# An mLSTM layer on one Trainium2 core: column blocks of the projections taken in pairs, five of eight k chunks by Strassen's seven products

## The chip, the cores and the metric

The kernel runs on one core of one Trainium2 chip. The metric is the device time of one execution in microseconds, as the median of several runs. Lower is better. The kernel before takes 1814.12 us (three runs, 1814.03 to 1814.68).

## The reference

One residual layer for 256 rows (tokens) of 4096 float32 numbers. The rows are normalised by their root mean square, multiplied by w_in (4096 x 16400), and the columns of the product are q and k (8 heads of 256 each), v, og and z (8 heads of 512 each) and 16 gate columns. After a small causal convolution on q and k comes an mLSTM step per head; its result is normalised, gated by sigmoid(og) and silu(z), multiplied by w_out (4096 x 4096) and added to x.

```
u = rms_norm(x) @ w_in
qk, v, og, z, ig, fg = split(u)                 # 2*2048, 4096, 4096, 4096, 8, 8 columns
q, k = silu(causal_conv(qk))                    # 8 heads of 256
a = exp(decay) * (q @ k.T) / 16                 # per head, causal
h = (a @ v) / max(|sum(a)|, exp(-m))            # 8 heads of 512
y = rms_norm_per_head(h) * w * sigmoid(og) * silu(z)
out = x + y @ w_out
```

Nearly all of the arithmetic is the two projections: 256 x 4096 x 20496 multiplications.

## The kernel before

Rows are two tiles of 128 (t = 0, 1), the 4096 of the contraction are 32 k tiles of 128, in 8 chunks of 4 (CK). Float32 accuracy is kept by splitting each operand into a high and a low part of 12 bits (`split`, lines 127 to 130: the high part is a copy on ACT, the low part a subtraction on DVE) and by three matmuls for each product (`matmul3`, lines 132 to 136: high x high, high x low, low x high).

`project` (line 165) computes one block of 512 columns (NB): for each chunk it loads 4 k tiles of weights by SP's DMA (1 MB, three buffers), splits two k tiles at a time (128 x 1024, lines 129 and 130, three buffers each of high and low parts), and issues 24 matmuls for them on TensorE. A block of 512 columns is 192 matmuls with 512 columns each, into two PSUM banks. The split x (the stationary side) stays in SBUF for the whole of w_in. The blocks come in the order of `column_blocks` (line 42): og and z of two heads, then q, k and v of the pair of heads. The first two blocks are computed side by side while x comes in; two blocks (gq, 272 columns, and q1, 256) and the last two of w_out (256) are narrow. In all there are 38 blocks of 512 columns, 31 of w_in (the first two among them) and 7 of w_out, and 4 narrow ones.

Work on finished blocks (convolution, `head` with its stages weights, values and turn, the gates) is put into a queue `stages`, and one stage is issued after each chunk of the blocks that follow. y goes through TensorE transposes into `yT` and is split by `split_y` to be the stationary side of w_out. The tile framework fixes the order of each engine's instructions before the run: where an instruction isn't ready by the framework's own reckoning it puts a later one ahead. Each engine then works in that fixed order.

Of the kernel before, what the change touches and what calls it, by code (L numbers as in the profile page):

```python
# [28 lines left out]
COLS = 2 * QK + 3 * INNER + 2 * HEADS  # L29
# [4 lines left out]
VW = DV + 2  # L34
CK = 4
SK = 2
WARM = 8
NPAIR = HEADS // 2
OUT_BLOCKS = [NB] * 7 + [NB // 2] * 2


def column_blocks():
    """Blocks of w_in's columns in the order in which they are used: (what, head or pair, spans)."""
    o_v, o_og, o_z, o_g = 2 * QK, 2 * QK + INNER, 2 * QK + 2 * INNER, 2 * QK + 3 * INNER
    blocks = []
# [12 lines left out]
    return blocks
# [3 lines left out]
def mlstm_layer(ctx: ExitStack, tc: tile.TileContext, x, xT, norm_w, w_in, conv_w, conv_b, gate_b,  # L62
# [3 lines left out]
    act_in = ctx.enter_context(tc.tile_pool(name="act_in", bufs=1))  # L66
    wpool = ctx.enter_context(tc.tile_pool(name="wpool", bufs=3))
    work = ctx.enter_context(tc.tile_pool(name="work", bufs=2))
    small = ctx.enter_context(tc.tile_pool(name="small", bufs=1))
    ps_pj = ctx.enter_context(tc.tile_pool(name="ps_pj", bufs=4, space=PSUM))  # L70
    ps_a = ctx.enter_context(tc.tile_pool(name="ps_a", bufs=2, space=PSUM))
    ps_n = ctx.enter_context(tc.tile_pool(name="ps_n", bufs=2, space=PSUM))

# [5 lines left out]
    # The array's clock rises while it is busy: products that nothing reads, until the first operands are there.  # L79
    idle = ps_n.tile([P, P], F32, name="idle", tag="n")  # L80
# [4 lines left out]
    # tri[s, t] = 1 where s <= t  # L85
# [4 lines left out]
    # maskT[s, t] = 0 where key s of a tile may be seen by query t of that tile and of the next  # L90
# [5 lines left out]
    nc.vector.tensor_scalar(nid, ident[:HEADS, :HEADS], -1.0, None, op0=OP.mult)  # L96

# [17 lines left out]
    def rsqrt(dst, src, n, tag):  # L115
        """dst = src ** -0.5 for [P, n] of positive float32."""
# [10 lines left out]
    def split(hi, lo, src):  # L127
        """src as hi + lo, each of 12 bits."""
        nc.scalar.activation(hi, src, AF.Copy)  # L129
        nc.vector.tensor_sub(lo, src, hi.bitcast(F32))  # L130

    def matmul3(ps, a, b, first=True, last=True):
        """ps (+)= a.T @ b of float32 operands given as (hi, lo)."""
        nc.tensor.matmul(ps, a[0], b[0], start=first, stop=False)  # L134
        nc.tensor.matmul(ps, a[0], b[1], start=False, stop=False)  # L135
        nc.tensor.matmul(ps, a[1], b[0], start=False, stop=last)  # L136

    # Work on finished blocks, in stages that are issued between the chunks of the blocks that follow.
    stages = deque()

    yT = act_in.tile([P, KT, T], F32, name="yT")

# [1 line left out]
    rstd = const.tile([P, NT], F32, name="rstd")  # L144
    ss_part = const.tile([P, NT, 4], F32, name="ss_part")

    def row_squares(t, c):
        xr = work.tile([P, D // 4], F32, name=f"xr_{t}_{c}", tag="G")
        nc.sync.dma_start(xr, x[t * P:(t + 1) * P, c * (D // 4):(c + 1) * (D // 4)])
        nc.scalar.activation(xr, xr, AF.Square, accum_out=ss_part[:, t, c:c + 1])  # L150

    def row_stats():
# [3 lines left out]
        rsqrt(rstd, ss, NT, "row")  # L156

# [1 line left out]
    def split_x(raw, hi, lo, c, j):  # L159
        s = nw[:, c * CK + j:c * CK + j + 1]  # L160
        nc.scalar.activation(hi[:, j, :], raw[:, j, :], AF.Copy, scale=s)
        nc.vector.scalar_tensor_tensor(lo[:, j, :], raw[:, j, :], s, hi[:, j, :].bitcast(F32),
                                       op0=OP.mult, op1=OP.subtract)

    def project(name, w, off, widths, lhs, start=False, between=None, end=False):
        """Column blocks of w side by side, from off on; returns the psum tiles of each."""
        ps = [[pool.tile([P, NB], F32, name=f"pj_{name}_{b}_{t}", tag=tag)[:, :width] for t in range(NT)]
              for b, (width, (pool, tag)) in enumerate(zip(widths, ((ps_pj, "pj"), (ps_n, "n"))))]
        for c in range(KT // CK):
            # k tiles that are loaded and split together; the first ones are small, to begin early  # L170
            loads = [(0, CK)]
            if start and c < 2:
                loads = [(0, 1), (1, SK), (SK, CK)] if c == 0 else [(0, SK), (SK, CK)]
            raws = []
            for b, width in enumerate(widths):
                raw = wpool.tile([P, CK, NB], F32, name=f"w_{name}_{b}_{c}", tag="wraw")
                raws.append(raw.rearrange("p a b -> p (a b)")[:, :CK * width])
            if start:
                xraw = work.tile([P, CK, T], F32, name=f"xT_{c}", tag="G")
                xsplit = [act_in.tile([P, CK, T], F32R, name=f"x{part}_{c}", tag=f"{part}{c}")  # L180
                          for part in ("hi", "lo")]
                lhs.append(xsplit)
            for a, z in loads:
                if start:
                    nc.sync.dma_start(xraw[:, a:z, :], xT[:, c * CK + a:c * CK + z, :])
                for b, width in enumerate(widths):
                    o = off + D * sum(widths[:b]) + c * CK * P * width + a * width
                    nc.sync.dma_start(raws[b][:, a * width:z * width],
                                      bass.AP(tensor=w.tensor, offset=w.offset + o,
                                              ap=[[CK * width, P], [1, (z - a) * width]]))  # L190
            n = 1 if start and c == 0 else SK * NB // max(widths) // 2 * 2
            for k0 in range(0, CK, n):
                if start:
                    for j in range(k0, k0 + n):
                        split_x(xraw, *xsplit, c, j)
                for b, width in enumerate(widths):
                    hi = wpool.tile([P, SK, NB], F32R, name=f"wh_{name}_{b}_{c}_{k0}", tag="whi")
                    lo = wpool.tile([P, SK, NB], F32R, name=f"wl_{name}_{b}_{c}_{k0}", tag="wlo")
                    hi, lo = (u.rearrange("p a b -> p (a b)")[:, :n * width].rearrange("p (a b) -> p a b", a=n)
                              for u in (hi, lo))  # L200
                    split(hi, lo, raws[b].rearrange("p (a b) -> p a b", a=CK)[:, k0:k0 + n, :])
                    order = [(j, t) for j in range(n) for t in range(NT)]
                    for j, t in sorted(order, key=lambda jt: jt[1]) if end else order:
                        k = k0 + j
                        a = [lhs[c][part][:, k, t * P:(t + 1) * P] for part in range(2)]
                        matmul3(ps[b][t], a, (hi[:, j, :], lo[:, j, :]), c == 0 and k == 0,
                                c == KT // CK - 1 and k == CK - 1)
            if between is not None:
                between(c)
            if stages:  # L210
                stages.popleft()()
        return ps

# [1 line left out]
    gate = {}  # L215

    def gates(ps):
# [23 lines left out]
        def sums():  # L241
            pB = ps_a.tile([P, NT, HEADS], F32, name="pB", tag="a")
# [6 lines left out]
        def maxima():  # L249
            pc = ps_a.tile([HEADS, T], F32, name="pc", tag="a")  # L250
# [6 lines left out]
        def floor():  # L257
            pm = ps_a.tile([P, NT, HEADS], F32, name="pm", tag="a")
# [5 lines left out]
        return [take, forget, sums, maxima, floor]  # L264

# [1 line left out]
    def conv_qk(ps, dst, i0, ct0, n):  # L267
        """ps[t]: [P, n * 128], the columns from ct0 * 128; dst: (hi, lo), [P, .., T], filled from i0."""
# [124 lines left out]
    for n, (what, who, spans) in enumerate(blocks):  # L393
        width = sum(w for _, w in spans)

        def between(c, n=n):
            if n == 0 and c >= 4:
                for t in range(NT):
                    row_squares(t, c - 4)
# [99 lines left out]
```

## Time and profile before

| | |
|---|---|
| median of 3 runs | 1814.12 us |
| span of the profiled execution, first to last instruction | 1812.6 us (1.5 us less than the median) |
| TensorE (PE) busy | 1805.7 us, 8474 matmuls |
| VectorE (DVE) busy | 965.0 us |
| ScalarE (ACT) busy | 848.8 us |
| GpSimd (POOL) busy | 9.4 us |
| moved by DMA | 354 MB, mean 195 GB/s |
| granted TensorE clock, mean | 0.999 |

How to read it: a busy time is the sum of the durations that the profiler gives, without overlaps, so an engine whose busy time is near the span leaves no room. Durations of matmuls overlap (a matmul of 512 columns is shown with 389 ns, but the next one starts after 227 ns), and so, less, do those of DVE and ACT. What an instruction costs its engine is therefore read from the distance of starts where several stand back to back.

### The profile page before, as it was taken

The numbers are of one execution on the slowest core, as the hardware profiler recorded it, in microseconds if no ns is written. First come the engines' busy times: TensorE is split into PE (matmuls) and PEld (weight loads), VectorE is DVE, ScalarE is ACT, GpSimd is POOL, SyncE is SP. The second block draws the span as 40 slices with busy tenths as digits, with TensorE's granted clock in tenths as the row PEclk, the third lists the DMA queues.
The fourth block names the chain that finished last, engine by engine and source line by source line (L and its number), as shares of the span: only waits on it lengthen the run. The fifth ranks groups of instructions, "written<-read, shape, count | busy, mean of one in ns | idle before, by whom it ended". The sixth has DMA issues, their size and how long they took to land.

```text
span 1812.6 us, 20931 instructions
## 1 busy us (share of the span) xinstructions
PE 1805.7 (100%) x8474; PEld 1510.6 (83%) x8474; DVE 965.0 (53%) x1133; ACT 848.8 (47%) x994; POOL 9.4 (1%) x24
## 2 busy tenths in 40 slices
PE   9999999999999999999999999999999999999999
PEld 7888988888888888888888888888888888888889
DVE  5644656554544665545456655454466754444443
ACT  6643545454444454444445544444445653333332
POOL 0000000000000000000000000000000000000000
PEclk9999999999999999999999999999999999999999
DMA  8854655545555555455555544555555466665654
GB/s 311 277 204 176 200 187 186 181 168 188 199 193 188 190 181 185 164 197 196 187 196 194 175 176 172 200 185 195 200 186 185 171 225 209 219 222 203 213 187 141
DMA packets 57089, 354.07 MB, mean 195 GB/s; under 512 B 6944, under 2 KB 8352, under 8 KB 18592
## 3 DMA queue, kind: packets, MB, share of 16 engines
q1 hardware_dynamic: 55584, 348.80, 54.8%
q0 software_dynamic: 1120, 3.67, 0.5%
q8 instruction: 66, 1.08, 0.2%
q10 hardware_dynamic: 288, 0.26, 0.0%
q14 instruction: 31, 0.25, 0.0%
HBM read 348.51 MB, written 4.19 MB: 195 GB/s over the span
## 4 chain that ended last, share of the span: by engine, by line
PE 99%; DMA 0%; SPq 0%; ACT 0%; DVE 0%; issue 0%
PE pj_v L135 7%; PE pj_o L136 6%; PE pj_o L134 6%; PE pj_o L135 6%; PE pj_v L136 6%; PE pj_v L134 6%; PE pj_og L135 6%; PE pj_og L134 6%; PE pj_og L136 6%; PE pj_z L135 6%; PE pj_z L136 6%; PE pj_z L134 6%; PE pj_k L135 3%; PE pj_k L134 3%; PE pj_k L136 3%; PE pj_q L135 3%
## 5 line engine op out<-in xcount | busy, mean ns | idle before, releaser
L130 DVE TENSOR_TENSOR wl_o<-w_o,wh_o 128x1024 fp32r<-128x1024 f32 x128 | 156.8, 1225 | 174.6 <-ACT wh_o L129 174.6
L129 ACT ACTIVATE wh_o<-w_o 128x1024 fp32r<-128x1024 f32 x128 | 135.8, 1061 | 206.8 <-PE pj_o L136 206.0
L130 DVE TENSOR_TENSOR wl_z<-w_z,wh_z 128x1024 fp32r<-128x1024 f32 x112 | 137.2, 1225 | 167.4 <-ACT wh_z L129 167.4
L130 DVE TENSOR_TENSOR wl_v<-w_v,wh_v 128x1024 fp32r<-128x1024 f32 x128 | 156.7, 1224 | 116.3 <-ACT wh_v L129 115.4
L135 PE MATMUL pj_o<-wl_o,yh 128*128 128x512 f32 (+1 forms) x576 | 210.5, 366 | 0.0
L136 PE MATMUL pj_o<-wh_o,yl 128*128 128x512 f32 (+1 forms) x576 | 210.5, 366 | 0.0
L130 DVE TENSOR_TENSOR wl_og<-w_og,wh_og 128x1024 fp32r<-128x1024 f32 x112 | 137.1, 1225 | 135.9 <-ACT wh_og L129 135.4
L129 ACT ACTIVATE wh_v<-w_v 128x1024 fp32r<-128x1024 f32 x128 | 135.6, 1060 | 154.6 <-PE pj_v L136 136.1
L135 PE MATMUL pj_v<-wl_v,xhi 128*128 128x512 f32 x512 | 202.4, 395 | 0.0
L136 PE MATMUL pj_v<-wh_v,xlo 128*128 128x512 f32 x512 | 199.9, 391 | 0.0
L129 ACT ACTIVATE wh_z<-w_z 128x1024 fp32r<-128x1024 f32 x112 | 118.8, 1061 | 169.5 <-PE pj_z L136 146.2
L129 ACT ACTIVATE wh_og<-w_og 128x1024 fp32r<-128x1024 f32 x112 | 118.8, 1060 | 160.7 <-PE pj_og L136 141.7
L134 PE MATMUL pj_o<-wh_o,yh 128*128 128x512 f32 (+1 forms) x576 | 193.3, 366 | 0.0
L134 PE MATMUL pj_v<-wh_v,xhi 128*128 128x512 f32 x512 | 183.7, 391 | 0.0
L135 PE MATMUL pj_og<-wl_og,xhi 128*128 128x512 f32 x448 | 175.0, 391 | 0.0
L136 PE MATMUL pj_og<-wh_og,xlo 128*128 128x512 f32 x448 | 174.4, 389 | 0.0
L135 PE MATMUL pj_z<-wl_z,xhi 128*128 128x512 f32 x448 | 174.3, 389 | 0.0
L136 PE MATMUL pj_z<-wh_z,xlo 128*128 128x512 f32 x448 | 174.3, 389 | 0.0
L134 PE MATMUL pj_og<-wh_og,xhi 128*128 128x512 f32 x448 | 158.3, 390 | 0.0
L134 PE MATMUL pj_z<-wh_z,xhi 128*128 128x512 f32 x448 | 156.1, 389 | 0.0
L136 PEld LDWEIGHTS pj_o<-wh_o,yl 128*128 128x128 f32 x576 | 108.7, 189 | 17.4
L134 PEld LDWEIGHTS pj_o<-wh_o,yh 128*128 128x128 f32 x576 | 108.7, 189 | 17.4
(174 smaller groups left out, 2984.5 us busy)
## 6 DMA issues: line engine op xcount, KB each, us to landing
w_v<-in_w_in SPq DMA_DIRECT2D x64, 1024.0 KB, 4.8
w_og<-in_w_in SPq DMA_DIRECT2D x56, 1024.0 KB, 4.8
w_z<-in_w_in SPq DMA_DIRECT2D x56, 1024.0 KB, 4.8
w_o<-in_w_out SPq DMA_DIRECT2D x56, 1024.0 KB, 4.9
w_k<-in_w_in SPq DMA_DIRECT2D x32, 1024.0 KB, 4.8
w_q<-in_w_in SPq DMA_DIRECT2D x24, 1024.0 KB, 4.8
w_first<-in_w_in SPq DMA_DIRECT2D x12, 1024.0 KB, 6.8
w_o<-in_w_out SPq DMA_DIRECT2D x16, 512.0 KB, 3.5
```

What stands on the lines that cost most here:

```text
L129: nc.scalar.activation(hi, src, AF.Copy)
L130: nc.vector.tensor_sub(lo, src, hi.bitcast(F32))
L134: nc.tensor.matmul(ps, a[0], b[0], start=first, stop=False)
L135: nc.tensor.matmul(ps, a[0], b[1], start=False, stop=False)
L136: nc.tensor.matmul(ps, a[1], b[0], start=False, stop=last)
```

## The change

w_in and w_out are now taken in pairs of column blocks (n1, n2) of 512 columns, 19 pairs: for each head q and k in n1 and v in n2 ("qkv"), and og in n1 and z in n2 ("oz"), and four pairs of w_out ("o"). The gates' columns and q, k, v of head 0 (1040 columns) are computed ahead in the old way, as x comes in. In 5 of the 8 k chunks (FAST) the two row tiles, the two halves of the chunk (2 k tiles each, HK) and the two blocks form a 2 x 2 block product, and that is done by seven block products in place of eight (P1 to P7, the variant with 4 sums of weights and 4 differences of x). Each of the seven has its own PSUM bank over the whole pair. The other three chunks are plain, eight block products a chunk, but added into the banks P2 to P5, with a difference of the row tiles ("D") as one of the stationary operands. At the end of a pair `combine` makes the four result blocks out of the seven banks with 4 copies on ACT and 7 sums on DVE.

The stationary sides (7 sums or 3, split) are built by `build` for each chunk, from normalised x (`build_x`) and later from y (`build_y`, which reads y back from DRAM). Of the four weight sums of a chunk two are additions on DVE (for P6 and P4) and two are DMAs that GpSimd issues with accumulation, DRAM added onto a tile in SBUF: after P1's split w12 is added onto the raw w11 (used by P5), and after the addition for P6 w12 is added onto the raw w22 (used by P7). Loads are now 512 KB each, with 7 raw buffers; split parts still have three buffers each. All attention steps share one PSUM bank ("m"). The row sums of a head are six small matmuls with a column of ones. The output's last adds come out of `combine`.

```diff
+FAST = (0, 1, 3, 4, 6)
+ORDER = ("P1", "P3", "P2", "P5", "P6", "P4", "P7")
+DSUM = 2
...
+    def build(c, src):
+        if c in FAST:
...
+            F = big(f"F_{c}", [P, 4, HK, P])
+            nc.vector.tensor_sub(F[:, 0], a21, a22)
+            nc.vector.tensor_sub(F[:, 3], a21, a11)
+            nc.vector.tensor_sub(F[:, 1], a11, F[:, 0])
+            nc.vector.tensor_sub(F[:, 2], a12, F[:, 1])
...
+                for a in range(s0, s1):
+                    split(L[:, 0, a], L[:, 1, a], v[:, a - s0])
...
+            nc.vector.tensor_sub(F, src[:, :, :P], src[:, :, P:])
+            for i, v in enumerate((src[:, :, :P], src[:, :, P:], F)):
+                split(L[:, 0, i], L[:, 1, i], v)
...
+    def build_x(c):
+        src = big(f"xn_{c}", [P, CK, T])
+        nc.sync.dma_start(src, xT[:, c * CK:(c + 1) * CK, :])
+        for j in range(CK):
+            k = c * CK + j
+            nc.vector.scalar_tensor_tensor(src[:, j, :], src[:, j, :], nw[:, k:k + 1], rstdB,
+                                           op0=OP.mult, op1=OP.mult)
+        build(c, src)
...
+        def made(s):
+            if s == "P1":
+                raw["11"] = load(f"{name}_{c}_11", w, at, n)
+            elif s == "P3":
+                raw["22"] = load(f"{name}_{c}_22", w, at + P * n, n)
+            elif s == "P2":
+                raw["21"] = load(f"{name}_{c}_21", w, at + 2 * P * n, n)
...
+            elif s == "P6":
+                if DSUM:
+                    nc.vector.tensor_add(raw["11"], raw["11"], raw["22"])
+                    nc.gpsimd.dma_start(raw["22"], source(w, at + 3 * P * n, n), accum_op=OP.add)
...
+            elif s == "P4":
+                if DSUM < 3:
+                    nc.vector.tensor_add(raw["21"], raw["21"], raw["11" if DSUM else "22"])
...
+            h = operand(f"{name}_{c}_{s}", src)
+            if DSUM and s == "P1":
+                nc.gpsimd.dma_start(src, source(w, at + 3 * P * n, n), accum_op=OP.add)
...
+    def project_pair(name, w, off, between=None):
+        ps = {s: bank(f"{s}_{name}", s) for s in TAGS}
+        fast = [u for c in FAST for u in fast_steps(name, w, off, c)]
+        plain = [u for c in range(NCH) if c not in FAST for u in plain_steps(name, w, off, c)]
+        steps = sorted([((i + 0.5) / len(fast), u) for i, u in enumerate(fast)]
+                       + [((i + 1) / len(plain), u) for i, u in enumerate(plain)], key=lambda v: v[0])
...
+    def combine(name, ps, xs=None):
...
+        for dst, s in ((p1, "P1"), (B[:, 0], "P3"), (B[:, 1], "P5"), (r7, "P7")):
+            nc.scalar.activation(dst, ps[s], AF.Copy)
+        tt(A[:, 0], ps["P2"], p1, op=OP.add)
+        tt(B[:, 0], B[:, 0], B[:, 1], op=OP.add)
+        tt(p1, ps["P6"], p1, op=OP.subtract)
+        tt(r7, r7, p1, op=OP.add)
+        tt(B[:, 0], B[:, 0], p1, op=OP.add)
+        tt(B[:, 1], B[:, 1], r7, op=OP.add)
+        tt(A[:, 1], ps["P4"], r7, op=OP.subtract)
...
+    for n, (what, h, _, _) in enumerate(pairs):
+        def between(c, share, n=n):
+            if builds and share * 8 > NCH - len(builds) - 5:
+                f, b = builds.popleft()
+                f(b)
+            if n == len(pairs) - 1 and c is not None and c < HEADS - 1:
+                build_y(c)
```

## Rows read from the trace of the kernel before

**Rows 1.** The page: busy time of each engine, clock by slice, and the chain.

```profile
PE 1805.7 (100%) x8474; PEld 1510.6 (83%) x8474; DVE 965.0 (53%) x1133; ACT 848.8 (47%) x994; POOL 9.4 (1%) x24
PEclk9999999999999999999999999999999999999999
...
PE 99%; DMA 0%; SPq 0%; ACT 0%; DVE 0%; issue 0%
```

**Rows 2.** Windows: stretch, length, busy of each engine, clock, DMA share, GB/s.

```profile
353.13:714.17 361.04, 361.04 (x1635) 298.91 (x1633) 192.52 (x226) 168.49 (x196) 0.00 (x0) 1.00 0.53 187
8.00:96.70 88.70, 88.67 (x383) 72.85 (x383) 55.23 (x84) 58.20 (x87) 0.00 (x0) 0.98 0.87 309
96.70:140.20 43.50, 43.50 (x193) 36.05 (x192) 22.24 (x21) 18.21 (x19) 0.00 (x0) 1.00 0.55 194
183.70:207.80 24.10, 24.10 (x193) 24.06 (x193) 13.90 (x20) 12.31 (x19) 0.00 (x0) 1.00 0.59 179
207.80:231.30 23.50, 23.50 (x199) 23.50 (x198) 15.23 (x20) 15.57 (x21) 0.00 (x0) 1.00 0.72 248
```

**Rows 3.** Timeline of DVE: start, us, instruction; xN are N back to back.

```profile
15.15 1.29 DVE L130 TENSOR_TENSOR wl_first<-w_first,wh_first 128x512 fp32r<-128x512 f32 x2 [0.59 <-ACT wh_first L129]
...
22.57 3.50 DVE L130 TENSOR_TENSOR wl_first<-w_first,wh_first 128x1024 fp32r<-128x1024 f32 x3 [0.47 <-ACT wh_first L129]
...
28.87 3.25 DVE L162 SCALAR_TENSOR_TENSOR xlo<-xT,nw,xhi 128x256 fp32r<-128x256 f32 x8
...
239.19 1.51 DVE L289 SCALAR_TENSOR_TENSOR acc<-pt,cw,acc 128x255 f32<-128x255 f32 x3
...
701.86 0.16 DVE L123 TENSOR_TENSOR rs_t_h<-rs_r_h 128x2 f32<-128x2 f32 x1
702.00 1.22 DVE L130 TENSOR_TENSOR wl_v<-w_v,wh_v 128x1024 fp32r<-128x1024 f32 x1
703.14 0.15 DVE L124 SCALAR_TENSOR_TENSOR rs_t_h<-rs_t_h,ss 128x2 f32<-128x2 f32 x1
703.33 0.16 DVE L125 SCALAR_TENSOR_TENSOR rs_r_h<-rs_t_h,rs_r_h 128x2 f32<-128x2 f32 x1
```

**Rows 4.** Groups of instructions by line: busy us, mean ns, idle before, releaser.

```profile
L129 ACT ACTIVATE wh_o<-w_o 128x1024 fp32r<-128x1024 f32 x128 | 135.8, 1061 | 206.8 <-PE pj_o L136 206.0 <-PE pj_v L136 0.8
L326 DVE SCALAR_TENSOR_TENSOR E<-pM,c,maskT 128x256 f32<-128x256 f32 (+1 forms) x16 | 5.9, 413 | 8.7 <-PE pM L319 8.7
L329 DVE SCALAR_TENSOR_TENSOR E<-pS,E 128x384 f32<-128x384 f32 x8 | 4.5, 557 | 7.5 <-PE pS L136 7.5
L462 DVE TENSOR_TENSOR o<-pj_o,o 128x512 f32<-128x512 f32 (+1 forms) x18 | 10.6, 624 | 6.1 <-PE pj_o L136 6.1
```

**Rows 5.** DMA issues: size of each, median us from issue to landing; then POOL's own time.

```profile
w_v<-in_w_in SPq DMA_DIRECT2D x64, 1024.0 KB, 4.8
...
w_o<-in_w_out SPq DMA_DIRECT2D x16, 512.0 KB, 3.5
...
out<-o POOLq DMA_DIRECT2D x14, 256.0 KB, 5.7
...
out<-o ACTq DMA_DIRECT2D x2, 128.0 KB, 2.7
...
1546.10 1.14 POOL L464 DMA_DIRECT2D out<-o  x2 [42.28 <-DVE o L462]
```

**Rows 6.** Timeline of all engines at the end of the span.

```profile
1808.96 0.28 PE L136 MATMUL pj_o<-wh_o,yl 128*128 128x256 f32 x1
1809.28 0.42 DVE L462 TENSOR_TENSOR o<-pj_o,o 128x256 f32<-128x256 f32 x1 [1.01 <-PE pj_o L136]
1809.73 0.34 ACTq L464 DMA_DIRECT2D out<-o  x1
```

**Rows 7.** Timeline of PE behind the first wait for weights.

```profile
9.61 0.63 PE L136 MATMUL pj_first<-wh_first,xlo 128*128 128x512 f32 x1
10.03 0.63 PE L135 MATMUL pj_first<-wl_first,xhi 128*128 128x512 f32 x1
...
12.48 0.39 PE L135 MATMUL pj_first<-wl_first,xhi 128*128 128x512 f32 x1
12.71 0.39 PE L136 MATMUL pj_first<-wh_first,xlo 128*128 128x512 f32 x1
```

More of the change, by code (lines that the diff above doesn't have):

```diff
@@ L17 @@
 PSUM = bass.MemoryType.PSUM
+DRAM = bass.MemoryType.DRAM
 P = 128
@@ L156, in row_stats @@
         rsqrt(rstd, ss, NT, "row")
[L159 to L207, printed above, removed]
-            if between is not None:
-                between(c)
-            if stages:
-                stages.popleft()()
-        return ps
@@ new lines, in project_pair @@
+    def project_pair(name, w, off, between=None):
[4 more added lines that the diff above has]
+                       + [((i + 1) / len(plain), u) for i, u in enumerate(plain)], key=lambda v: v[0])
+        total = len(fast) + 2 * len(plain)
+        uses = {s: len(FAST) * HK for s in TAGS}
+        for s in ("P2", "P3", "P4", "P5"):
+            uses[s] += (NCH - len(FAST)) * CK
+        seen = dict.fromkeys(TAGS, 0)
+        left = {c: 7 if c in FAST else 4 for c in range(NCH)}
+        done = popped = 0
+        for _, (c, make, cost) in steps:
+            for s, prods in make():
+                for a, b in prods:
+                    seen[s] += 1
+                    matmul3(ps[s], a, b, seen[s] == 1, seen[s] == uses[s])
+            left[c] -= 1
+            done += cost
+            if between is not None:
+                between(c if left[c] == 0 else None, done / total)
+            if done * NCH >= (popped + 1) * total:
+                popped += 1
+                if stages:
+                    stages.popleft()()
+        return ps
@@ new lines, in mlstm_layer, with head, decay @@
+    V = [lhs_pool.tile([P, NT, DV], F32R, name=f"v{part}") for part in range(2)]
+    y = {}
+    def head(h):
+        qT, kT = qk
+        A = [work.tile([P, 3 * P], F32R, name=f"A{part}_{h}", tag=f"A{part}") for part in range(2)]
+        E = work.tile([P, 3 * P], F32, name=f"E_{h}", tag="E")
+        spans = ((0, 0, T, 0), (1, T, 3 * P, P))
+        r = small.tile([P, NT], F32, name=f"r_{h}", tag="r")
+        ss = small.tile([P, NT], F32, name=f"ss_{h}", tag="ssh")
+        s2 = small.tile([P, NT], F32, name=f"s2_{h}", tag="s2", bufs=2)
+        def decay():
+            pM = misc(f"pM_{h}", [P, T])
@@ L350, in values, with rows @@
+        def rows():
+            pq = misc(f"pq_{h}", [P, NT, 2])
+            for t in range(NT):
+                mm = [(a, part) for a, _ in terms[t] for part in range(2)]
+                for n, (a, part) in enumerate(mm):
+                    nc.tensor.matmul(pq[:, t, :], A[part][:, a * P:(a + 1) * P], onesr, start=n == 0,
+                                     stop=n == len(mm) - 1)
+            nc.scalar.activation(r, pq[:, :, 0], AF.Abs)
             nc.vector.tensor_max(r, r, gate["enm"][:, :, h])
@@ L378, in head, with last @@
-        return [weights, values, turn]
-    ylhs = {}
-    def split_y(c):
-        hi = act_in.tile([P, CK, T], F32R, name=f"yh_{c}", tag=f"hi{c}")
-        lo = act_in.tile([P, CK, T], F32R, name=f"yl_{c}", tag=f"lo{c}")
-        split(hi, lo, yT[:, c * CK:(c + 1) * CK, :])
-        ylhs[c] = (hi, lo)
-    lhs = []
-    off = 0
-    G, qk, sgo = {}, {}, {}
-    blocks = column_blocks()
[L393 to L397, printed above, removed]
-                for t in range(NT):
-                    row_squares(t, c - 4)
-            if n == len(blocks) - 1 and c >= 2:
-                split_y(c - 2)
-        if n == 0:
-            both = project("first", w_in, off, [width, width], lhs, True, between)
+        def last():
+            values(1)
+            scale()
@@ new lines, in finish, with turn, run @@
+        def finish(G):
+            for t in range(NT):
+                nc.vector.scalar_tensor_tensor(y[h][:, t, :], y[h][:, t, :], s2[:, t:t + 1], G[:, t, :],
+                                               op0=OP.mult, op1=OP.mult)
+        return [decay, weights, rows, lambda: values(0), last], finish
+    spill = {}
+    def turn(h):
+        yT = {}
+        def run(i):
+            if i == 0:
+                yT[0] = big(f"yT_{h}", [P, CK, T])
+            py = misc(f"py_{h}_{i}", [P, 2, T])
+            for a in range(2):
+                for t in range(NT):
+                    nc.tensor.transpose(py[:, a, t * P:(t + 1) * P], y[h][:, t, (2 * i + a) * P:(2 * i + a + 1) * P],
+                                        ident)
+            for a in range(2):
+                k = h * CK + 2 * i + a
+                nc.scalar.activation(yT[0][:, 2 * i + a, :], py[:, a, :], AF.Copy, scale=onw[:, k:k + 1])
+            if i == 1:
+                if h == HEADS - 1:
+                    build(h, yT[0])
+                else:
+                    spill[h] = dram.tile([P, CK, T], F32, name=f"spill_{h}", tag=f"spill{h}")
+                    nc.gpsimd.dma_start(spill[h], yT[0])
+        return [lambda: run(0), lambda: run(1)]
@@ new lines, in mlstm_layer @@
+    for n in range(D // (2 * NB)):
+        cols = [slice((2 * n + i) * NB, (2 * n + i + 1) * NB) for i in range(2)]
+        ps = project_pair(f"o{n}", w_out, n * D * 2 * NB)
+        xs = []
+        for i in range(2):
+            xo = big(f"xo_{n}_{i}", [P, NT, NB])
+            for t in range(NT):
+                nc.sync.dma_start(xo[:, t, :], x[t * P:(t + 1) * P, cols[i]])
+            xs.append(xo)
+        res = combine(f"o{n}", ps)
+        for i in (1, 0):
+            for t in range(NT):
+                nc.vector.tensor_add(xs[i][:, t, :], xs[i][:, t, :], res[i][:, t, :])
+                eng = nc.gpsimd if n < 3 else (nc.sync, nc.scalar)[t]
+                eng.dma_start(out[t * P:(t + 1) * P, cols[i]], xs[i][:, t, :])
```

418 lines of the change are left out of this document (243 added, 175 removed).

## The prediction

> **What bounds the kernel now.** I read the page first: PE is busy for the whole span, at full clock in every slice, and the chain of waits is 99% PE [rows 1]. The groups of instructions agree: ACT, which makes the high parts of the weights, stands idle mostly because it waits for PE to free a buffer [rows 4]. So time is a number of matmuls by their pace, and the windows give the pace [rows 2]: a block of 512 columns takes 43.5 us for its 192 matmuls, 226.6 ns each; the narrow ones take 24.1 us (272 columns) and 23.5 us (256), 0.125 us a matmul. From one head pair's transposes to the next pass 361.0 us; less eight blocks (348.0) this leaves 13.0 for the attention work of two heads, 6.5 a head. DVE is busy for about half of this time (192.5 of 361.0), and in the densest long stretch, the first 89 us, for 62%. DMA moved 309 GB/s there, against 187 later.
>
> **Matmuls removed.** Before: 38 x 43.5 + 24.1 + 3 x 23.5 = 1747.6 us. After, a pair of blocks has 5 x 7 x 2 x 3 = 210 matmuls in the fast chunks and 3 x 48 = 144 in the plain ones, 354 where two old blocks have 384: 80.2 us. 19 pairs take 1523.8, the columns ahead 24.1 + 23.5 + 43.5 = 91.1, together 1614.9. Saved: 132.7 us. A head's six row sums and the nine wide matmuls that replace eighteen narrow ones add about 0.5 us a head, 4 in all. The floor by PE is 1812.6 - 132.7 + 4 = 1684.
>
> **The end.** Today 3.6 us pass from the last matmul's start to the end [rows 6]. After: the last plain step ends P2 and P4; behind it stand two sums from PSUM (0.62 each, the nearest row is the last add of today [rows 4]), up to four adds of 0.6 [rows 3] and a 256 KB store, between 2.7 (128 KB, ACT's queue) and 5.7 (POOL's) [rows 5]. About 8, so +4: 1688.
>
> **What DVE gets.** I use distances of starts [rows 3]: 128x1024 costs (3.50 - 1.23)/2 = 1.14, 128x512 0.60, 128x256 (3.25 - 0.48)/7 = 0.40, a convolution tap 0.515, a small dependent one 0.20. A fast chunk has seven low parts and two additions, a plain one four low parts: 5 x 9 + 3 x 4 = 57 of 1.14 = 64.8 us, and `combine` has seven of about 0.62: 69.1 us for each pair, beside 80.2 us of PE. ACT has 47 high parts and four copies: 47 x 1.06 + 2.5 = 52 [rows 4], never the later. The whole of DVE's work comes to 1600 us: 19 x 69.1 = 1313; heads 8 x 15.1 (V 1.2, convolutions 2 x (6 x 0.515 + 1.2) = 8.6, decay and weights 1.9 [rows 4], row statistics 3.4); gating 8 x 3.5 (2 x 1.14 + 2 x 0.60); x and y sides 71; the columns ahead 50; the rest 17. That is 95% of the PE floor. It only fits if it is spread, and it isn't:
> - "oz" pairs of heads 1 to 6 carry the head's 15.1: 84.2 us of DVE beside 80.2 + 5.2 = 85.4 of PE. Each low part waits for its high part, so I let DVE reach 95%: 88.6, +3.2 each, +19. If it reached 100%, 0; at 85%, +14 each.
> - the first "oz" pair also builds chunks 5 to 7 of the x side (6 + 2 x 4: normalising 4 x 0.40; fast 11 x 0.40, plain 4 x 0.60) and the gates (2.5): 99.5/0.95 = 105 against 85.4, +19.
> - the last "oz" pair builds seven chunks of the y side, 5 x 4.4 + 2 x 2.4 = 26.8: 111/0.95 = 117, +31.
> - the columns ahead: in their last three chunks (34.2 us of PE) DVE has 18.6 of its own, the row statistics (4) and five chunks of the x side (28): 50.6/0.95 = 53, +19.
> - "qkv" and "o" pairs have DVE at 72.6 of 81.9 and 71.8 of 80.2: nothing added; if waits bite there too, 2 us for each of 11, 22.
> Sum +88 (ends 0 and 88 + 64 + 22): 1776.
>
> **Accumulating DMAs.** No row of before shows one. Each is issued when DVE has read the tile, and the next reader (ACT's copy for P5, or for P7) stands in ACT's fixed order; behind it wait DVE's low part and, once the three buffers are used up, PE. Let L be the time from the issue until the data is there. Without any reordering a fast chunk is a ring: L, P5's high and low part (2.3), the addition (1.1), L again, P7's and the next P1's parts (3.5), some 1.1 for signals: 2L + 8. PE gives a fast chunk 84.5/5 = 16.9 us, so L up to 4.4 is hidden even then. The nearest rows are 3.5 us (a 512 KB load) and 5.7 (a 256 KB store by POOL), plus POOL's own 0.57 for each [rows 5]: L between 3.5 and 6.3, more if reading the old value doubles the transfer. At 6.3 the ring is 20.6: 3.7 us for each of 95 chunks. But the order need not be that of the code: the trace shows a later weight tile's low part put between two steps of one head's rsqrt chain [rows 3], so the next plain step or the next chunk's P1 can be put ahead of P5, and then only DVE's total counts. I take 0 and keep 350 as the far end. The bytes are no bound: 16.8 MB of a pair, 2.6 more as w12 is loaded twice, and the 5.2 of old values read make 24.6 MB in 87 us, 283 GB/s, under the 309 that the trace shows. POOL's queue has 190 x 0.57 = 108 us of it in all, with only a spill or a store between; loads stay on SP's queue as before.
>
> The Trainium skill ("DMA: Bandwidth & Descriptors", section "Anatomy of one DMA — SWDGE (gpsimd) path") fits a DMA issued from GpSimd by about 2.0 us and its bytes at 436 GB/s. By that, an estimate, 512 KB are there after 3.2 us and the ring would hide them in any order; by the row of POOL's store, 5.7 us for half the bytes, it would not, so the trace disagrees with the rule here.
>
> **Other edits.** Seven product banks have no second copy: the next pair's P2 needs one DVE sum behind the last matmul (0.65 + 0.2) and comes two steps (2.7 us) later, P4 comes seven steps later; hidden as long as DVE isn't 2 us behind. If it is, 1 to 2 us for each of 18 changes, 36 at most. The single bank for attention only delays stages, of which one is issued in 10 us. y goes to DRAM and back (512 KB, 3.5 us each way) a head before it is needed: 0.
>
> **Sum.** 1776 in the profile's span; the median stood 1.5 above it: 1778.
>
> **Rivals.**
> 1. All of it hides: 1688 + 1.5 = 1690. For it: DVE's total is under PE's. Against it: the four stretches above in which DVE has more than PE.
> 2. The accumulating DMAs take PE's place as the bound: a fast chunk lasts 2L + 8, in the order of ACT's copies for P5 and P7. It decides from L = 4.4 without reordering; 0.4 us a chunk more than my sum (38 us over 95 chunks) already makes the change slower than before. At L = 6.3 and with half of the wait filled by other steps: 1778 + 95 x 1.4 = 1911; with none filled about 2030 (the overflows of DVE hide in it). For it: POOL's 5.7 us for half the size. Against it: the 3.5 us of a load, and the order that the trace shows.
> 3. DVE is the bound all over: 1600 us divided by the share that it can be kept busy. My sum is 90%; 88% is no gain, 85% is 1882 (slower). For it: no stretch of before shows more than 62%. Against: there DVE waited for PE's buffers or loads, not for itself.
> 4. PE's gaps cost it its clock: behind the first wait for weights matmuls stand 0.43 us apart at the half clock (1.2 GHz), later 0.23 [rows 7]. If the first and the last "oz" pair ran so, 80 us more each, 1938. Against: the gaps there are a fifth of the time in small pieces, and 3 us later the matmuls stood 0.23 us apart.
> The Trainium skill ("TensorE: Matmul & The Clock Gate", section "HAM oscillation — how this bites in real kernels") tells of a kernel that lost the clock at each wait for data. By that rule rival 4 would strike; the trace has one such place, at the start.
>
> **Chances.** My sum (1740 to 1812) 0.47; rival 1 (1690 to 1740) 0.12; a tie 0.06; rival 2 0.19; rival 3 0.12; rival 4 0.04. A difference under 0.2% (3.6 us) can't be told from none. Faster: 0.47 + 0.12 = 0.59; same 0.06; slower 0.35. The range reaches down to 1700 and up to 1900, which leaves out the worst of rivals 2 and 4 and the best of rival 1, some 0.16 together. The likeliest's own range is 1740 to 1812.
>
> **What would show it.** Right: matmuls 227 ns apart, 354 for each pair; pair times of 80 to 82 us in w_out, 82 to 84 for "qkv", 87 to 90 for "oz", 100 to 117 for the first and last "oz"; PE's share of the span near 95% and DVE's over 90% in the "oz" pairs; idle time of PE released by DVE's low parts. Wrong: ACT idle for its copies of P5 and P7 with a DMA as the releaser (rival 2); DVE waiting for ACT's high parts for more than a tenth of a "qkv" or "o" pair (rival 3); a granted clock under 0.97 behind the start (rival 4); pairs of 80 us all over (rival 1).

## The result and the profile after

The kernel after takes 2238.39 us (median of 4 runs, 2231.85 to 2244.04) against 1814.4: a ratio of 1.2334 (95% interval 1.231 to 1.2357). The forecast was 1778, in a range of 1700 to 1900. The profiled execution took 2237.44 us with a span of 2235.7.

The page of after, the lines that answer to [rows 1]:

```profile
PE 1905.8 (85%) x7690; PEld 1450.4 (65%) x7690; DVE 1611.3 (72%) x1839; ACT 1168.5 (52%) x1368; POOL 174.9 (8%) x219
...
PEclk9989999999999999999999999999999999898989
...
issue 9%; DMA 8%; DVE 4%; ACT 1%; PE 1%; POOL 0%; POOLq 0%; ACTq 0%; DVEq 0%
```

PE is no longer the chain (99% before, 1% now; the chain could be followed through 23% of the span only), and no engine is full: PE 85, DVE 72 and ACT 52%. That is what a ring of waits would look like. The windows of after (columns as in [rows 2]), first a "qkv" pair, then an "o" pair:

```profile
1107.00:1218.00 111.00, 92.77 (x360) 70.54 (x359) 74.56 (x68) 55.23 (x58) 8.87 (x11) 0.92 0.64 175
...
1889.00:2001.00 112.00, 93.78 (x352) 70.29 (x350) 73.46 (x68) 50.17 (x51) 10.83 (x14) 0.91 0.67 189
```

Both last 111 to 112 us, where 82 and 80 were forecast, although their work outside the projections differs. Between the first pair and the last "oz" pair every "qkv" pair takes 108 to 113 us and every "oz" pair, which has the most work for DVE, 106 to 109: something common to all pairs sets the time. 112/5 is 22 us for a fast chunk. The groups of after for ACT's high parts (answering to the first of [rows 4]) name the releaser:

```profile
L134 ACT ACTIVATE wh_oz_P<-w_oz 128x1024 fp32r<-128x1024 f32 x280 | 294.5, 1057 | 316.8 <-DMA w_oz<-in_w_in 167.5 <-PE P_oz L141 50.0 <-DVE w_oz L249 43.6
...
L134 ACT ACTIVATE wh_qkv_P<-w_qkv 128x1024 fp32r<-128x1024 f32 x245 | 256.6, 1056 | 359.3 <-DMA w_qkv<-in_w_in 210.7 <-DVE w_qkv L249 67.5 <-PE P_qkv L141 45.4
...
L134 ACT ACTIVATE wh_o_P<-w_o 128x1024 fp32r<-128x1024 f32 x140 | 146.8, 1057 | 218.5 <-DMA w_o<-in_w_out 117.4 <-DVE w_o L249 46.7 <-PE P_o L141 38.8
```

Before, ACT waited for PE [rows 4]. Now it waits 495.6 us for DMAs and 157.8 for DVE's sum of P6 (L249). All of the 495.6 are accumulating DMAs: who waited for P1's (source line L263, us and times) and below it for P6's (L250), each with the time from issue to landing, that is, until the data is there:

```profile
  ACT wh_qkv_P L134: 132.3, 32
  ACT wh_oz_P L134: 91.1, 37
  ACT wh_o_P L134: 77.8, 18
...
DMA to landing us min/median/max: 5.1/7.0/9.5
...
  ACT wh_qkv_P L134: 78.4, 30
  ACT wh_oz_P L134: 76.4, 32
  ACT wh_o_P L134: 39.6, 15
...
DMA to landing us min/median/max: 5.1/5.4/7.5
```

The chain of after in one "o" pair (start, us, what) shows how they hang together:

```profile
1910.14 9.35 DMA w_o<-in_w_out
...
1919.60 1.06 ACT wh_o_P L134
1920.69 1.24 DVE wl_o_P L135
1921.95 1.24 DVE w_o L249
1923.21 0.51 issue
1923.74 0.09 POOL w_o L250
1923.83 9.69 issue
1933.53 7.89 DMA w_o<-in_w_out
...
1941.53 1.06 ACT wh_o_P L134
...
1955.95 5.94 DMA w_o<-in_w_out
...
1961.99 1.06 ACT wh_o_P L134
```

This is the ring that the prediction wrote down and then set to nothing. P1's tile gets its accumulating DMA (9.35 us on the chain); then come P5's high part and low part, the addition for P6, POOL's second DMA (its landing lies in the 9.69 us that the chain calls issue, with P7 and the next chunk's P1 behind it), and the next chunk's first DMA at 1933.53. P5's copies stand at 1919.60, 1941.53 and 1961.99: 21.9 and 20.5 us a chunk. In the timeline of ACT the wait stands in front of P5, and nothing is put before it. The copy behind it, of a plain step, needs no wait of its own (the number in brackets is idle time, and who ended it):

```profile
1934.98 1.06 ACT L134 ACTIVATE wh_o_P<-w_o 128x1024 fp32r<-128x1024 f32 x1 [0.53 <-PE P_o L141]
1941.53 1.06 ACT L134 ACTIVATE wh_o_P<-w_o 128x1024 fp32r<-128x1024 f32 x1 [5.48 <-DMA w_o<-in_w_out]
1942.49 1.04 ACT L134 ACTIVATE wh_o<-w_o 128x1024 fp32r<-128x1024 f32 x1
```

The DMA issues of after (median from issue to landing, answering to [rows 5]) and its queues (packets, MB, share of 16 engines):

```profile
q1 hardware_dynamic: 91680, 307.13, 38.5%
q0 software_dynamic: 29328, 106.44, 27.3%
...
w_oz<-in_w_in SPq DMA_DIRECT2D x216, 512.0 KB, 4.7
...
w_oz<-in_w_in POOLq DMA_DIRECT2D x80, 512.0 KB, 5.5
w_qkv<-in_w_in POOLq DMA_DIRECT2D x70, 512.0 KB, 5.6
w_o<-in_w_out POOLq DMA_DIRECT2D x40, 512.0 KB, 5.5
```

So L is 5.5 us by the median of all, inside the forecast bounds of 3.5 and 6.3; but by place it is 7.0 for P1's DMA, above them, and 5.4 for P6's.

The waits also cost clock. PE behind the wait of the chain at 1941.5, in windows of 2 us (clock in the third column from the end) and in the timeline:

```profile
1940.00:1942.00 2.00, 0.25 (x2) 0.00 (x0) 0.00 (x0) 0.47 (x1) 0.00 (x0) 1.00 0.07 20
1942.00:1944.00 2.00, 0.91 (x3) 0.48 (x3) 1.38 (x2) 1.53 (x2) 0.00 (x0) 1.00 0.00 0
1944.00:1946.00 2.00, 2.00 (x8) 1.58 (x8) 2.00 (x2) 0.00 (x0) 0.00 (x0) 0.68 0.04 6
1946.00:1948.00 2.00, 2.00 (x6) 1.61 (x5) 1.97 (x3) 1.57 (x2) 0.85 (x1) 0.50 0.76 256
1948.00:1950.00 2.00, 2.00 (x10) 1.54 (x9) 1.77 (x2) 1.00 (x2) 0.00 (x0) 0.97 0.89 125
```

```profile
1945.53 0.63 PE L139 MATMUL P_o<-wh_o,lhs 128*128 128x512 f32 x1
1945.95 0.63 PE L140 MATMUL P_o<-wl_o,lhs 128*128 128x512 f32 x1
...
1948.35 0.40 PE L141 MATMUL P_o<-wh_o,lhs 128*128 128x512 f32 x1
1948.58 0.40 PE L139 MATMUL P_o<-wh_o,lhs 128*128 128x512 f32 x1
```

PE had 1.2 us of work between 1940 and 1944, still at full clock, and in the stretch behind it, to about 1948, its matmuls stood 0.43 us apart (1.2 GHz) as in [rows 7], then 0.23 again. Over the whole trace 402 of 6725 distances of the projections' matmuls lie between 0.415 and 0.47 us. At 0.20 each above the usual 0.23 that is about 80 us of PE's time. As PE is busy for 85% of the span only, how much of it is in the 424 us that the change loses is not shown.

### The profile page after: what moved, and what is told of

It reads as the page before. It is cut to its first block, busy times and chain, and to the rows that moved or that the text cites. A ratio compares the mean times of both kernels' runs of the same rounds, so it can differ in the third digit from the quotient of the medians.

```text
span 2235.7 us, 22156 instructions
## 1 busy us (share of the span) xinstructions
PE 1905.8 (85%) x7690; PEld 1450.4 (65%) x7690; DVE 1611.3 (72%) x1839; ACT 1168.5 (52%) x1368; POOL 174.9 (8%) x219
## 3 DMA queue, kind: packets, MB, share of 16 engines
q0 software_dynamic: 29328, 106.44, 27.3%
## 5 line engine op out<-in xcount | busy, mean ns | idle before, releaser
L134 ACT ACTIVATE wh_oz_P<-w_oz 128x1024 fp32r<-128x1024 f32 x280 | 294.5, 1057 | 316.8 <-DMA w_oz<-in_w_in 167.5
L135 DVE TENSOR_TENSOR wl_qkv_P<-w_qkv,wh_qkv_P 128x1024 fp32r<-128x1024 f32 x245 | 297.5, 1223 | 225.2 <-ACT wh_qkv_P L134 224.5
L135 DVE TENSOR_TENSOR wl_oz_P<-w_oz,wh_oz_P 128x1024 fp32r<-128x1024 f32 x280 | 341.6, 1221 | 154.9 <-ACT wh_oz_P L134 154.3
L134 ACT ACTIVATE wh_qkv_P<-w_qkv 128x1024 fp32r<-128x1024 f32 x245 | 256.6, 1056 | 359.3 <-DMA w_qkv<-in_w_in 210.7
L139 PE MATMUL P_oz<-wh_oz_P,lhs 128*128 128x512 f32 x560 | 236.7, 427 | 78.4 <-ACT wh_oz_P L134 77.0
L139 PE MATMUL P_qkv<-wh_qkv_P,lhs 128*128 128x512 f32 x490 | 208.4, 431 | 104.1 <-ACT wh_qkv_P L134 103.5
L140 PE MATMUL P_oz<-wl_oz_P,lhs 128*128 128x512 f32 x560 | 236.2, 422 | 15.0 <-DVE wl_oz_P L135 14.9
L141 PE MATMUL P_oz<-wh_oz_P,lhs 128*128 128x512 f32 x560 | 229.6, 410 | 0.0
L140 PE MATMUL P_qkv<-wl_qkv_P,lhs 128*128 128x512 f32 x490 | 206.6, 422 | 5.1 <-DVE wl_qkv_P L135 5.0
L141 PE MATMUL P_qkv<-wh_qkv_P,lhs 128*128 128x512 f32 x490 | 202.4, 413 | 0.0
L139 PE MATMUL P_oz<-wh_oz,lhs 128*128 128x512 f32 x384 | 147.7, 419 | 12.5 <-ACT wh_oz L134 12.5
L141 PE MATMUL P_oz<-wh_oz,lhs 128*128 128x512 f32 x384 | 153.3, 399 | 0.0
L139 PE MATMUL P_qkv<-wh_qkv,lhs 128*128 128x512 f32 x336 | 135.7, 431 | 13.7 <-ACT wh_qkv L134 13.5
L141 PE MATMUL P_qkv<-wh_qkv,lhs 128*128 128x512 f32 x336 | 134.0, 399 | 0.0
```

## The experiments

Each kernel was timed beside the kernel before on the same chip (1814.5 to 1814.9); ratios are to that.

### Is it the wait for the accumulating DMAs?

**e14.** The loads, DMAs, additions and matmuls stay in number and size; P5, P6, P7 and P4 read tiles that no accumulating DMA writes.

```diff
-                    nc.vector.tensor_add(raw["11"], raw["11"], raw["22"])
-                    nc.gpsimd.dma_start(raw["22"], source(...), accum_op=OP.add)
+                    nc.vector.tensor_add(raw["22"], raw["22"], raw["21"])
+                    nc.gpsimd.dma_start(raw["11"], source(...), accum_op=OP.add)
...
-            src = raw[{..., "P5": "11", "P6": "11" ...
+            src = raw[{..., "P5": "22", "P6": "22" ...
```

> The change (five fast chunks, order of the code, the same loads, accumulating DMAs, additions and matmuls in number and size), but P5, P6, P7 and P4 take tiles that no accumulating DMA writes, so that no split waits for one; the two DMAs of a chunk both add into the tile of P1, which nobody reads then. Left out by it: the sums that belong to P5, P6, P7 and P4. Theory (the ring through the two landings is what the change loses): pairs fall from 111-113 us to 85-92, where DVE and three operand buffers set them, 1780-1900. Rival (the accumulating DMAs cost by their load on the 16 engines and by the lower clock, not by a wait for them): above 2000.

Measured: 1931.42 us, ratio 1.0637 (1.0618 to 1.0656). A little above the expected 1900, below the rival's 2000. So 307 of the 424 us come with the wait, the clock that it costs among them (granted 0.973 here, 0.938 in the kernel after): the DMAs themselves still run, with the same landings (7.1 and 5.4 us by place). ACT still waits for DVE's sum of P6 (58.4, 51.4 and 35.8 us in the three kinds of pair, 146 in all) and for 41 us for that of P4.

**e16, e17.** e14 with the two DVE sums of a chunk put behind the last reader of their tile; e17 with a fourth buffer for high parts, paid for by the seventh weight buffer.

```diff
-                    nc.vector.tensor_add(raw["22"], raw["22"], raw["21"])
...
+            if s == "P4":
+                nc.vector.tensor_add(src, src, raw["22"])
+            if s == "P7":
+                nc.vector.tensor_add(src, src, raw["21"])
```

> e14_no_wait with the two DVE sums of a chunk moved behind the last reader of the tile that they write (P4's and P7's split), so that no split waits for a sum either; as many instructions as before, of the same sizes. Left out: the weight sums that P5, P6, P7 and P4 need. Theory (the order of a chunk's own steps, not DVE's total, is what e14 still loses against the forecast of 1778): ACT no longer waits for DVE's sums (146 us in e14), pairs of 80-87, 1730-1830. Rival (DVE's total and the handshake of three operand buffers): 1880-1930.

> e16_no_chain with four buffers for high parts and, for space, six for loaded weights. If three operand buffers are what e16 has left: 30-60 us less than e16. If DVE's total is: within 15 us of e16. If loads then come late for want of a buffer: more than e16, with DMA as the releaser of ACT.

Measured: e16 1837.21 (1.0119; 1.0102 to 1.0137); e17 1849.14 (1.0176; 1.0154 to 1.0198): the missing weight buffer costs more than the operand buffer gives, with DMA as the releaser of ACT for 56.9 us in the plain steps of the "oz" pairs. e16's time is 7 us above the theory's range and 43 below the rival's: 94 us more were the waits for the chunk's two sums, which e16 takes away together. Windows of e16, a "qkv" and an "oz" pair:

```profile
1101.00:1186.30 85.30, 83.91 (x364) 66.73 (x363) 75.18 (x69) 56.11 (x58) 9.11 (x12) 1.00 0.82 229
1186.30:1277.10 90.80, 88.08 (x392) 70.52 (x391) 82.74 (x104) 61.41 (x71) 8.47 (x11) 1.00 0.76 216
```

With the waits for landings and sums inside a chunk gone, and the same work, the "qkv" and "oz" pairs come close to the forecast (82 to 84, 87 to 90).

### Does the ring follow the landing time?

**e2.** The same DMAs write in place of adding (the two sums that they make are left out).

```diff
-                    nc.gpsimd.dma_start(raw["22"], source(...), accum_op=OP.add)
+                    nc.gpsimd.dma_start(raw["22"], source(...))
```

> The changed kernel with the same 190 DMAs from GpSimd at the same places, but they overwrite the tile and don't add to it (the two sums are left out). Every wait stays. Ring theory: time falls only by what the landing gets shorter: from 7.0 and 5.4 us to perhaps 5 and 4, 3.4 us for each of 95 chunks, 320 us at most; 1920 to 2150 us, and ACT still waits for these DMAs in each chunk. Rival, the DMA engines (accumulating costs them twice the time a byte, 27.3% of 16 engines for 106 MB, and holds up the loads): their share falls by some 13 points and the time goes below 1900 us. Nothing but the wait matters: 2200 us or more.

Measured: 2009.6 (1.1075; 1.1053 to 1.1097), inside the ring theory's range. The landing falls from 5.5 to 4.4 us:

```profile
q0 software_dynamic: 29328, 106.44, 15.8%
...
w_o<-in_w_out POOLq DMA_DIRECT2D x40, 512.0 KB, 4.4
```

By place it falls from 7.0 to 4.8 us (P1's) and from 5.4 to 3.8 (P6's), 3.8 us a ring; the change of the total, 229 us over 95 chunks, is 2.4. ACT's wait for DMAs in the fast steps falls from 495.6 to 195.5 us. The time follows the landings, but not one for one. By itself e2 can't tell the wait from the load on the DMA engines, which falls as well; e14 can, where the load stays.

### Can the order fill it?

**e3, e12.** The same work; P1, P3 and P2 of the next chunk stand between P5, P6, P4 and P7 of this one. e12 has a fourth buffer for high parts and one weight buffer less.

```diff
+            n1, n3, n2 = ([u] for u in by_chunk[i + 1][:3]) if i + 1 < len(FAST) else ([], [], [])
+            fast += [p5, p6] + n1 + [p4] + n3 + [p7] + n2
```

> The changed kernel with the same work, the same DMAs and the same 7 raw buffers; only the order of the products is another: P1, P3 and P2 of the next fast chunk are put between P6, P4, P7 of the one before and so ahead of its own P5. Between a DMA and its reader there are then four products (P1 to P5) and three (P6 to P7) in place of two and one, and the two DMAs run side by side. Ring theory: a chunk lasts about L + 5 = 13 us, less than PE's 16.9, so the wait goes away; 1780 to 1900 us, the granted clock back to over 0.97. Rival, the DMA engines: they do the same work, so 2150 us or more. Rival, the clock alone: no change either.

> e3_two_chunks (1995) with four buffers for high parts, and six for loaded weights in place of seven for space. If what e3 still loses is the handshake of three buffers: 1890-1950. If it is DMA and order: 1970-2010, or above with the buffer less.

Measured: e3 1995.23 (1.1; 1.0979 to 1.102): missed, but 243 us better by order alone; ACT waits for DMA 135.5 us in place of 495.6. e12 2021.95 (1.1145; 1.1123 to 1.1168): as in e17, the weight buffer is missed more, and ACT waits for DMA 279.7 us in the fast steps.

**e15, e11.** Four fast chunks and four buffers for high parts, in the order of the code (e15) and in e3's (e11).

```diff
-FAST = (0, 1, 3, 4, 6)
+FAST = (0, 2, 4, 6)
```

> e11_dma4_hi4 (1823.5) in the order of the code. With 28 fast steps among 16 plain ones two fast steps and 1.7 plain ones, 7.5 us of PE's work, lie between P1 and P5, against a landing of 5.5 us, a split, an issue and two semaphores: about 1 to 3 us late in each ring, 80 chunks: 1840-1920 by the ring theory; 1810-1830 if order no longer matters at this spacing.

> Four fast chunks, accumulating DMAs, the interleaved order of e3_two_chunks, four buffers for high parts. Room theory: pairs of 83-85, 1755-1800, faster than before. Rival (DMA still releases ACT in each chunk): 1830-1900.

Measured: e15 2004.6 (1.1047; 1.1031 to 1.1063), e11 1823.53 (1.0053; 1.0035 to 1.0071). Order alone is worth 181 us here. Both missed: e15 lies 85 us above its range, e11 24 above its 1800.

### Sums on another engine

**e1, e5.** All four weight sums of a chunk on DVE (e1; P7's sum takes another tile than needed, same size), or on POOL (e5), w12 as a fourth load.

```diff
-DSUM = 2
+DSUM = 0
```

In e5 also, with P5's sum issued behind P1's split and the other three behind P5's:

```diff
-                    nc.vector.tensor_add(raw["11"], raw["11"], raw["12"])
+                add(raw["P1"], raw["P1"], r12)          # add = nc.gpsimd.tensor_add
```

> The changed kernel with all four weight sums of a fast chunk on DVE and w12 as a fourth load; no accumulating DMA is left. Ring theory (the time from issue to landing of two accumulating DMAs, one behind the other in ACT's order, sets 22.6 us for each fast chunk): without them a pair goes down from 111 us to what DVE needs, (47 + 20) x 1.14 + 4.3 = 81 us in the w_out pairs and some 95 in the oz pairs; 1850 to 1950 us in all. Rival, the clock (the array lost its clock for reasons of its own, granted 0.938): over 2100 us, as nothing is done for it. Rival, DVE (it is the bound in any case): slower than 2238, as DVE gets 190 more additions of 1.22 us.

> As e1_dve_sums (five fast chunks, no accumulating DMA), but all four weight sums of a fast chunk are POOL additions, 20 a pair, issued as soon as the parts are split. Theory (after the DMA wait is gone, what e1 loses is DVE's: 20 sums of 1.14 us a pair): the pairs fall from e1's 92.5 us to 82-86, 19 x 8 = about 150 us, to 1780-1830. Rival (the order of the code is the trouble: P5 and P6 wait for a sum that starts only when P1 is split): if a POOL addition takes 2.5 us or more, three of them in a row stand in the ring of a chunk, POOL becomes the releaser of ACT, and pairs take 95-110, 2000-2250.

Measured: e1 1958.3 (1.0792; 1.0771 to 1.0814), slightly above its range; DVE is now at 1800.0 us, 92% of the span. e5 2465.36 (1.3586; 1.3563 to 1.3608): the rival, and worse than it. Groups of e5:

```profile
L135 DVE TENSOR_TENSOR wl_oz_P<-w_oz_P,wh_oz_P 128x1024 fp32r<-128x1024 f32 x280 | 425.2, 1531 | 122.5 <-ACT wh_oz_P L134 121.5
...
L248 POOL TENSOR_TENSOR w_oz_P<-w_oz_P,w_oz 128x1024 f32<-128x1024 f32 x40 | 121.5, 3037 | 0.0
```

A POOL addition takes 2.5 to 3.1 us by the means of its groups where DVE takes 1.22, and DVE's own low parts went from 1.22 to 1.53 us in this group, and to 1.9 to 2.1 in plain steps.

**e6, e8.** Three fast chunks, sums and four of combine's additions on POOL; e8 with a fourth buffer for high parts.

> Three fast chunks as e4_three_fast, weight sums on POOL and four of combine's seven additions on POOL. Theory (DVE late, above all in the first 15 us of a pair where combine, the additions to x and the sums meet): DVE work falls by 16 us a pair, the stalls of PE for low parts (about 6 us a pair) go, pairs 84-86, 1740-1790: faster than before. Rival (the 6 us are the handshake of three operand buffers between ACT, DVE and PE, whatever DVE's load): 1850-1870 as e4.

> e6 and e7 together. By either theory the low parts are no longer late: pairs at 84-85, 1735-1780. If it stays above 1814, what is lost is not in the pairs but in the start (first columns, building of chunks) and in the heads.

Measured: 2075.23 (1.1431; 1.1414 to 1.1448) and 1960.13 (1.0802; 1.0785 to 1.0818). Both missed, with e5's signs: ACT waits for POOL's sum of P6 for 126 and 168 us, and in e6 DVE's low parts take 1.4 to 2.0 us on the mean.

### Fewer fast chunks, so that plain steps fill the ring

**e4, e7, e10.** Sums on DVE: three fast chunks (e4; P7's sum as in e1); the same with P7's sum made in P6's step and four buffers for high parts (e7); four fast chunks (e10).

```diff
-        hi = wpool.tile([P, RAW], F32R, name=f"wh_{name}", tag="whi")[:, :n]
+        hi = wpool.tile([P, RAW], F32R, name=f"wh_{name}", tag="whi", bufs=4)[:, :n]
```

> All four sums on DVE, and only 3 of 8 chunks by seven products. PE: 366 matmuls a pair in place of 384, 1812.6 - 77.5 + 8 = 1743 us; DVE has (3 x 11 + 5 x 4) x 1.14 + 4.3 = 64.7 us beside 83 of PE, 78%. Ring theory and PE as the bound: 1750 to 1800 us, faster than before. If DVE's waits for ACT's high parts are the bound (rival 3 of the prediction): slower than 1814.

> As e4_three_fast (sums on DVE, in the order that gives the reference's result), with four buffers for high parts in place of three. Handshake theory: ACT no longer stands between PE's release and DVE's low part, so 1.2 us is taken out of each ring, 1790-1840. DVE-load theory: the stalls stand where DVE is saturated for 15 us, one buffer does little: 1855-1875.

> e7_hi4 (1814.6) with four fast chunks: 6 matmuls fewer a pair (-1.4 us), 7 DVE instructions of 1.14 us more (+8). Handshake theory (with the fourth buffer PE no longer waits for DVE as long as DVE's sum is below PE's): 1785-1800. DVE theory (DVE is full in stretches, each instruction more there is late work): 1815-1860.

Measured: e4 1871.85 (1.0316; 1.0301 to 1.0331), e7 1814.58 (0.9998; 0.9989 to 1.0007), e10 1851.41 (1.0201; 1.0186 to 1.0217). e4 missed by 72 us. e7 agrees with its handshake theory, but the sum's place changed with the buffer, so its 57 us can't be put down to the buffer. e10 agrees with the DVE theory: 8 us more of DVE a pair cost 37 us in all.

**e13, e9.** The change with three fast chunks and nothing else (e13), and with four buffers for high parts (e9).

```diff
-FAST = (0, 1, 3, 4, 6)
+FAST = (0, 3, 6)
```

> The change with three fast chunks in place of five, nothing else (e9_dma3_hi4 with three buffers for high parts). Room theory: the landings are hidden already, the fourth buffer is worth what it was with sums on DVE (e4 to e7: 57 us) or less: 1800-1855. Rival (the fourth buffer is what hid them): 1900 or more.

> The change as it is (accumulating DMAs, order of the code), with three fast chunks in place of five and four buffers for high parts. Theory (the time lost is the ring P1 - DMA - P5 - P6 - DMA - P7, which has no room when 35 fast steps stand among 12 plain ones): among 21 fast and 20 plain steps some 11 us of PE's work lie between P1 and P5, the landing of 5.5 us is hidden, ACT waits for DMA under 40 us in all, and DVE has two sums a chunk less than in e7_hi4: 1785-1815. Rival (every accumulating DMA costs PE some us wherever it stands, by its load on the 16 engines): 114 of them, 1860 or more.

Measured: e13 1812.75 (0.9992; 0.9982 to 1.0001): 12 matmuls more a pair, and 426 us less than the change. e9 1795.83 (0.9894; 0.9877 to 0.991): faster than the kernel before by 18.9 us. The buffer alone is worth 17. The page of e9 and its windows of a "qkv" and an "oz" pair:

```profile
PE 1769.2 (99%) x7918; PEld 1441.9 (80%) x7918; DVE 1400.1 (78%) x1621; ACT 1061.3 (59%) x1238; POOL 109.5 (6%) x143
...
PE 95%; DVE 2%; ACT 1%; DMA 1%; issue 1%; SPq 0%; DVEq 0%; ACTq 0%
```

```profile
1087.20:1172.90 85.70, 85.63 (x375) 69.39 (x374) 63.76 (x59) 49.43 (x52) 5.66 (x7) 1.00 0.73 222
1173.00:1263.10 90.10, 90.10 (x404) 73.39 (x403) 73.11 (x94) 55.18 (x65) 5.11 (x6) 1.00 0.69 204
```

PE is the chain again, at full clock, with 114 accumulating DMAs of the same size in the code's order: among 21 fast and 20 plain steps there is room between P1 and P5. ACT still waits 56 us for DMAs in the fast steps, where under 40 were expected.

## Why the prediction was wrong

**The step that failed** stands in the part on the accumulating DMAs: "But the order need not be that of the code ... I take 0 and keep 350 as the far end." The order was that of the code: from 1917 to 1964 ACT's copies come as `project_pair` lists the steps, and ACT stands idle in front of P5 with a plain step's copy behind it that then runs without a wait. What the tile framework put ahead elsewhere, it did not put ahead here. The row that I leaned on [rows 3] shows a low part put between small DVE instructions; it shows nothing about a step put ahead of one that waits for a DMA. The ring formula that I set aside gives 7.0 + 5.4 + 8 = 20.4 us with the measured landings, against 16.9 of PE: with it the sign was already slower. The runs: 307 us for the two landings (e14), 94 for ACT's waits for the two sums (e16), which in my sum stand only in DVE's total. That leaves 1837 against 1778.

**The size of the ring** was 20.5 to 22 us in the "o" pair: P1's DMA took 5.9 to 9.4 us there, where 6.3 was the upper bound, and POOL needs 0.85 us for an issue, not 0.57. Over the span: 2235.7 less the 112 us ahead of the first pair is 111.8 for each of 19 pairs, 22.4 for a fast chunk; what makes the 2 us above 20.4 was not settled.

**Rival 2 came true**, beyond its own price: 2030 with none of the wait filled. (Its 1911 goes by 1.4 us a chunk, where half of 3.7 is 1.85.) It had the place. Its point of decision, L = 4.4, is not borne out: e2's ring would be 4.8 + 3.8 + 8 = 16.6 us, under 16.9, and e2 is still 11% slower, with 149 us in which ACT waits for P6's sum. The rival had P6's addition at 1.1 us, but neither P4's sum nor the clock nor a landing of 7.0. Rival 4 came as its consequence, not by itself: a granted clock of 0.938, about 80 us of PE's time.

**Matmuls removed**: 354 a pair, as counted. Their pace was 0.23 us (the last lines of the PE timeline) and not 0.227; over some 6700 that is 20 to 25 us, also in e9, and no run tells why.

**What DVE gets**: 1611 us against 1600 forecast. The spread over the stretches was nearly right once nothing waits: in e16 112.8 us to the first pair (forecast 116: 91 + 19 and the start), 106 for the first "oz" pair (105), 112 for the last (117), 90 to 91 for the others (88.6). The "qkv" pairs take 85 to 90 against 81.9, some 29 us in all, of which the pace explains about 10. The "o" pairs were the furthest off: 90 to 91 each against 80 to 82, the last one with the end of the kernel in it, about 34 us in all. The stretches that came out shorter than forecast hide some of this in the 59 us that are left. DVE is at 76 of 91 us in the "o" pairs, so it is not full; what holds them was not settled.

**The end**: +4 forecast; 9.5 us now from the last matmul shown to the end against 3.6, so +6.

```profile
2226.24 0.40 PE L141 MATMUL P_o<-wh_o,lhs 128*128 128x512 f32 x1
...
2231.04 0.68 DVE L623 TENSOR_TENSOR xo<-xo,A_o 128x512 f32<-128x512 f32 x1
2231.16 0.94 ACTq L625 DMA_DIRECT2D out<-xo  x2
```

**Bytes** were no bound on the mean: the DMA engines were busy for 0.64 and 0.67 of the two windows of after, at 175 and 189 GB/s. The forecast's 283 can't be set beside these, as it has the old values, which the profile doesn't count (q0 shows 106.44 MB with and without adding). But the load came in bursts, which I hadn't priced: from 1905 to 1917, with P1's DMA under way beside the loads, the engines' share was 0.95 to 1.06, and from 1919 to 1925 0.10 or less. How much of the 7.0 us that makes, no run tells.

## What to carry to other kernels

Totals of engines give a time only where the work can be ordered freely: write down the ring from a tile's first reader through each landing and sum to its last reader, and compare it with the work that the code's order puts beside it. A reordering counts only if a row shows it past the very kind of wait in question. The cheapest cure was not a faster transfer but more independent steps between issue and use: with three fast chunks of eight the same kind of DMAs cost PE almost nothing, with four or five in the code's order they held it up.

## What the runs showed of the hardware

An accumulating DMA holds the DMA engines twice as long: q0's 106.44 MB took 27.3% of 2235.7 us, 5.73 us of all 16 engines a MB, against 15.8% of 2008.1, 2.98 us a MB, for the same transfers without adding (e2) and 2.80 for SP's loads. The Trainium skill ("Collectives: The Full Stack", section "The bandwidth ceiling: the fold count and why AG ≠ RS ≠ AR") explains a ratio of 1.93 in another setting by the two source reads that an add needs; the ratio here is 1.92.

Additions on POOL slowed DVE's two-input subtractions from 1.22 to 1.53 us on the mean and more (e5). The Trainium skill ("SBUF — State Buffer", section "Who interferes with whom") has such instructions contend for a shared read interface; the trace agrees that they do. Between 1100 and 1150 us of e5 six low parts started inside a POOL addition, and each ended 1.1 us behind that addition's end (one of 2.78 us from 1130.89 beside POOL's 2.40 from 1130.18), about the 1.21 that one takes alone: as if it had waited for the end.

The half clock did not come in the wait of the chain but behind it: the granted clock was 1.00 from 1940 to 1944, where PE had next to nothing to do, and 0.50 from 1946 to 1948, where it was full again. Behind the wait before that one, from 1918.1 to 1920.7, it was 0.50 from 1921 to 1927.
